# Half of the first weight quarter moved from the float32 queues to GpSimd's queue, with other warm-up matmuls

## The chip, the cores and the metric

One core of one Trainium2 chip. The metric is the device time of one execution in microseconds (us). The kernel before takes 903.51 us in the median of 3 runs (903.43 to 903.68). TensorE multiplies, VectorE (DVE), ScalarE (ACT) and GpSimd (POOL) do the rest, and SyncE (SP) issues transfers. SP and ACT have each a queue of transfers that move data as it is (q1 and q10 in the profile); GpSimd has one that can change the type on the way (q0).

## The reference: what is computed

```python
B, S, D = (16, 2048, 1024)
xw = x @ w                      # x [B, S, D], w [D, D], float32
out[:, 0, :] = xw[:, 0, :]
for t in range(1, S):
    out[:, t, :] = decay * out[:, t - 1, :] + xw[:, t, :]
```

A matrix product, and along the sequence a recurrence with one decay for each of the 1024 output columns.

## The kernel before

**Tiles.** x is cut into 64 chunks of 512 time steps (`TL`). The contraction of 1024 is cut into 8 slices (`K`), indexed k; k = 2m + e, with m = 0 to 3 and e = 0 (even) or 1 (odd). The 1024 output columns are 8 tiles n of 128; h = 0 or 1 is the half of w with n = 0 to 3 or 4 to 7. So w has four quarters (h, e), each of 512 KB in bfloat16 and 1 MB in float32; a quarter has four pieces m of 128 partitions x 512 columns.

**x.** `load` (L101) is issued on GpSimd and converts float32 to bfloat16; a chunk comes as four transfers, one for each quarter q of the partitions. `turn` (L110, DVE) transposes blocks of 32 x 32 pairs into xw; `part` (L119, ACT or DVE copy) makes xt from it. Matmuls of the first chunks read xw itself for some k (strided pairs) and xt for the others.

**w.** `load_w` (L317) brings one quarter (h, e) as four transfers, one for each 32 partitions, into a staging tile; `settle` (L324) copies one piece m into wsb, where the matmuls read it. The first quarter (0, 0) is called for at L334, on the SP and ACT queues in turn. These do not convert, so it arrives as float32, and `settle` casts it. The other three come on GpSimd's queue (`load_part`, L359) already as bfloat16.

**The order at the start** is written by hand in `agenda[-99]` (L532); each letter with its number is one entry of `deeds`:

- M0, M1: x's chunk 0 in two cuts, time blocks 0 to 9 and 10 to 15 of 16; M2, M3: chunk 1 in two halves. Four transfers each on GpSimd.
- U0, U1, U2: the quarters (0, 1), (1, 0), (1, 1) of w. Four transfers each on GpSimd.
- W or w with i: `settle` of piece i % 4 of quarter i // 4, on DVE (W) or ACT (w). 0 to 3 are the first quarter.
- K3: `spin_on(3)`, an ACT copy of one column of x's last quarter of partitions into gate (L356), and a matmul that nobody reads, behind it.
- E0 to E3: DVE transposes of the first cut, one for each m; G or F: the copies to xt on ACT or DVE. E4 and on: the following cuts.

GpSimd carries out its transfers' issues in this order, and DVE and ACT their copies in it. A GpSimd transfer takes one of eight semaphores in turn, so the ninth issue waits for the landing of the first.

**TensorE's order.** First `spin(5, seed, wide)` (L346): matmuls on zeros in float32, each two passes (10 in the profile), written to spare, which is not read. They wait for seed, whose first column ACT writes (L337) after it has loaded its table. Then the spin of K3; then step 0 (L652): for the first cut the even k = 0, 2, 4, 6 for four tiles n each (they read xw and the first quarter of w), then the odd k (xt and U0's quarter), and the same for the second cut, then chunk 1. From there on TensorE goes through steps of one tile n and two chunks each.

Of the kernel before, what the change touches and what calls it, by code (L numbers as in the profile page):

```python
# [9 lines left out]
FP32 = mybir.dt.float32  # L10
BF16 = mybir.dt.bfloat16
# [3 lines left out]
def _ap(ap_obj: bass.AP, new_ap, extra_offset=0):  # L15
    return dataclasses.replace(
        ap_obj,
        ap=[list(p) for p in new_ap],
        offset=ap_obj.offset + extra_offset,
    )  # L20
# [5 lines left out]
def kernel(  # L26
# [26 lines left out]
    nc = tc.nc  # L53
    pin = tc.keep_in_program_order
    B, S, D = x.shape
    assert w.shape == (D, D)

    NQ = 4
    P = 32
    CQ = D // NQ  # L60
    K = CQ // P
    M = K // 2
# [3 lines left out]
    R = K // 2  # L66
    CH = D // 2
    CR = CH // NQ

    const = ctx.enter_context(tc.tile_pool(name="const", bufs=1))  # L70
# [9 lines left out]
    def quad(q):  # L80
        return slice(q * P, (q + 1) * P)
# [12 lines left out]
    def ot_tile(nj):  # L94
        return ring(sb, "ot", 4, [128, nj, CR])
# [45 lines left out]
    class Tile:  # L141
# [45 lines left out]
        def copy(self):  # L187
            self.xs = sb.tile([128, 2 * TL], FP32, name=f"xs{self.lot % 3}")[:, 0:self.T]
            size = self.T // len(self.parts())
            for i, ps in enumerate(self.parts()):  # L190
                pin(nc.scalar.copy(out=self.xs[:, i * size:(i + 1) * size], in_=ps))  # L191
# [94 lines left out]
    class Outlet:  # L286
# [8 lines left out]
        def store(self, b, t0):  # L295
# [4 lines left out]
            for j in range(0, self.nj, nj):  # L300
# [8 lines left out]

    room = [ot_tile(2 * NJ).rearrange("p j c -> p (j c)") for _ in range(2)]  # L310
    size = M * CH
    stage = {(0, 0): room[0][:, 0:size],
             (0, 1): room[0][:, size:size * 3 // 2].bitcast(BF16),
             (1, 0): room[1][:, 0:size // 2].bitcast(BF16),
             (1, 1): room[1][:, size // 2:size].bitcast(BF16)}

    def load_w(queues, h, e):  # L317
        for i, q in enumerate((0, 2, 1, 3)):
            pin(queues[i % len(queues)].dma_start(  # L319
                out=stage[h, e][quad(q)].rearrange("p (m d) -> p m d", m=M),  # L320
                in_=_ap(w, [[2 * D, P], [2 * P * D, M], [1, CH]],
                        (q * CQ + e) * D + h * CH)))

    def settle(h, e, m, copy):  # L324
        src = stage[h, e][:, m * CH:(m + 1) * CH]
        pin(copy(out=wcols[:, 2 * m + e, h],  # L326
                 in_=src.rearrange("p (q r i) -> p q r i", q=NQ, r=R)))

    wide = const.tile([128, TL], FP32, name="wide")
    idle = wide[:, 0:TL // 2].bitcast(BF16)  # L330
    spare = ring(psp, "spare", 1, [128, TL])
    rows = const.tile([128, 2, P], FP32, name="rows")
    seed = const.tile([128, 128], FP32, name="seed")
    load_w((nc.sync, nc.scalar), 0, 0)  # L334
    pin(nc.vector.memset(wide, 0.0))
    pin(nc.vector.memset(seed, 0.0))
    pin(nc.scalar.copy(out=seed[:, 0:1], in_=wide[:, 0:1]))  # L337

    gate = const.tile([128, 128], BF16, name="gate")
    pin(nc.vector.memset(gate, 0.0))  # L340

    def spin(count, by, on):
        for _ in range(count):
            pin(nc.tensor.matmul(out=spare, lhsT=by, rhs=on, start=True, stop=True))  # L344

    spin(5, seed, wide)  # L346
    H = NJ // 2
    cuts = (((0, H + 2), (H + 2, NJ)), ((0, H), (H, NJ)))
    cols = const.tile([128, 2, P], FP32, name="cols")
# [7 lines left out]
        spin(1, gate, idle)  # L357

    def load_part(i):  # L359
        load_w((nc.gpsimd,), *((0, 1), (1, 0), (1, 1))[i])  # L360

    def part_one(i, copy):
        part(i // 8, copy, i % 4, i % 4 + 1, *cuts[i // 8][i // 4 % 2])
# [1 line left out]
    def settle_one(i, copy):  # L365
        settle(i // 8, i // 4 % 2, i % 4, copy)
# [119 lines left out]
    def turn_and_load(c):  # L486
# [16 lines left out]
        "w": lambda i: settle_one(i, nc.scalar.copy),  # L503
        "M": load_half,
        "U": load_part,
        "r": await_settled,
        "E": lambda i: turn(i // 8, *cuts[i // 8][i // 4 % 2], i % 4, i % 4 + 1),
# [21 lines left out]
        "L": lambda i: load(*loads.pop(0)) if loads else None,  # L529
    }  # L530
    agenda = {
        -99: "M0 U0 M1 M2 M3 U1 U2 w0 W1 w2 W3 K3 E0 E1 G0 E2 G1 E3 F2 G3 W4 w5 W6 W7 E4 E5 G4 E6 G5 E7 F6 G7 R E8 E9 G8 E10 G9 E11 F10 G11 E12 L E13 G12 L E14 G13 E15 L F14 G15 D",  # L532
        0: "",
        1: "",
        2: "",
# [220 lines left out]
```

## Time and profile before

| what | value |
|---|---|
| median of 3 runs | 903.51 us |
| the profiled execution | 903.32 us |
| its span, first to last instruction | 901.5 us |
| granted TensorE clock, mean | 0.999 |
| TensorE busy (PE) | 894.6 us, 99% |
| weight loads (PEld) | 412.8 us, 46% |
| DVE, ACT, POOL busy | 825.8, 685.7, 656.8 us |
| read from HBM, written to it | 138.42 MB, 134.22 MB |
| first spin on TensorE | 3.21 us |
| first real matmul (even k, first cut) | 10.90 us |
| first matmul of the odd k | 13.29 us |

Times inside the execution count from the start of the span. In the timeline, a line holds the start, the length, the engine, the line of the code, the operation, the tiles (out<-in) and the count of merged instructions; the brackets hold the engine's idle time before it and what ended that. PE is a matmul, PEld a weight load. In the view of the DMA queues a row holds packets, MB, and the time of the packets as a share of 16 engines' time. A queue's MB count what is written to the destination.

### The profile page before, as it was taken

Reading aid. Unit: us, or ns where it says so; the run is one execution under the profiler, and the core shown is the slowest. Engines: PE = TensorE matmul, PEld = TensorE weight load, DVE = VectorE, ACT = ScalarE, POOL = GpSimd, SP = SyncE. Lnnn points to the kernel's source line nnn. Section 1 sums busy time; section 2 is a strip of 40 time slices with the busy share of each in tenths; the row PEclk is TensorE's granted clock in tenths of the full one; section 3 lists DMA queues with packets and bytes.
Section 4 is the critical chain, followed back from the end, with each engine's and each line's share of the span. In section 5 each row is a group of like instructions: output and inputs, shape, how many; then the busy total and the mean of one; then the engine's idle time right before and its main releaser. Section 6 shows DMA issues by size and latency. Waiting matters only on the chain.

```text
span 901.5 us, 12309 instructions
## 1 busy us (share of the span) xinstructions
PE 894.6 (99%) x4211; PEld 412.8 (46%) x4211; DVE 825.8 (92%) x633; ACT 685.7 (76%) x957; POOL 656.8 (73%) x758
## 2 busy tenths in 40 slices
PE   8999999999999999999999999999999999999998
PEld 5544444444444444444444444444444444444444
DVE  4999989999999999999998999989999999999998
ACT  4888879877877877878778778777787787787743
POOL 7887778877767768677677687777777777776532
PEclk9999999999999999999999999999999999999999
DMA  9999999999999999999999999999999999999658
GB/s 189 192 211 244 244 205 215 215 230 240 248 237 264 242 254 242 256 253 246 220 245 218 228 241 211 239 223 228 236 228 223 229 235 226 230 219 219 187 135 239
DMA packets 403182, 204.77 MB, mean 227 GB/s; under 512 B 9392, under 2 KB 402096, under 8 KB 403120
## 3 DMA queue, kind: packets, MB, share of 16 engines
q0 software_dynamic: 137024, 68.70, 57.5%
q1 hardware_dynamic: 265808, 134.77, 57.1%
q8 instruction: 33, 0.54, 0.2%
q10 hardware_dynamic: 288, 0.52, 0.2%
q14 instruction: 29, 0.24, 0.1%
HBM read 138.42 MB, written 134.22 MB: 302 GB/s over the span
## 4 chain that ended last, share of the span: by engine, by line
PE 99%; ACT 0%; ACTq 0%; DVE 0%; DVEq 0%; issue 0%
PE ps L131 97%; PE spare L131 1%; PE spare L344 1%; ACT L337 0%; PE spare L412 0%; ACTq L319 0%; PE ps L412 0%; DVE h L440 0%; ACT seed L337 0%; DVEq L751 0%
## 5 line engine op out<-in xcount | busy, mean ns | idle before, releaser
L131 PE MATMUL ps<-xt,wsb 128*128 128x512 bf16 (+2 forms) x4040 | 865.9, 377 | 0.0
L131 PEld LDWEIGHTS <-wsb 128*128 128x128 bf16 x4184 | 408.3, 98 | 477.2 <-DVE wsb L326 0.3
L205 POOL TENSOR_TENSOR xs<-h,xs 128x512 f32<-128x512 f32 (+1 forms) x190 | 242.4, 1277 | 185.5 <-ACT h L171 84.4
L191 ACT COPY xs<-ps 128x1024 f32<-128x1024 f32 (+1 forms) x190 | 188.7, 994 | 153.4 <-PE ps L131 147.2
L278 DVE STREAM_TRANSPOSE ot<-so 128x1024 f32<-128x1024 f32 (+2 forms) x264 | 300.6, 1176 | 2.7 <-POOL so L266 2.0
L266 POOL TENSOR_TENSOR so<-h,xs 128x512 f32<-128x512 f32 (+1 forms) x189 | 240.6, 1274 | 38.4 <-ACT h L171 26.2
L123 ACT COPY xt<-xw 128x2048 bf16<-128x2048 bf16 (+3 forms) x136 | 242.4, 1788 | 5.8 <-DVE xw L115 5.8
L105 POOL DMA_DIRECT2D xb<-in_x_dram x264 | 173.8, 659 | 7.6 <-DMA xb<-in_x_dram 2.8
L171 ACT ACTIVATE h<-so,dec 128x512 f32<-128x512 f32 (+1 forms) x189 | 144.7, 766 | 26.6 <-DVE so L210 23.3
L115 DVE STREAM_TRANSPOSE xw<-xb 128x2048 f32<-128x2048 f32 (+3 forms) x78 | 147.2, 1899 | 6.1 <-DMA xb<-in_x_dram 6.1
L210 DVE TENSOR_TENSOR_SCAN so<-spare,keep,xs 128x512 f32<-128x512 f32 (+1 forms) x97 | 120.0, 1240 | 27.5 <-POOL xs L205 26.9
L210 DVE TENSOR_TENSOR_SCAN so<-spare,xs 128x512 f32<-128x512 f32 x93 | 113.3, 1220 | 25.9 <-POOL xs L205 22.6
L171 ACT ACTIVATE h<-ps,dec 128x512 f32<-128x512 f32 (+1 forms) x190 | 129.6, 683 | 0.0
L229 DVE TENSOR_TENSOR_SCAN so<-dec,ps 128x1024 f32<-128x1024 f32 x34 | 76.9, 2261 | 0.8 <-ACT h L171 0.6
L229 DVE TENSOR_TENSOR_SCAN so<-dec,keep,ps 128x1024 f32<-128x1024 f32 (+2 forms) x35 | 75.5, 2156 | 0.8 <-PE ps L131 0.8
L270 ACT COPY keep<-so 128x1 f32<-128x1 f32 x136 | 25.3, 188 | 9.3 <-DVE so L229 8.7
L201 ACT COPY so<-keep 128x1 f32<-128x1 f32 x97 | 18.3, 191 | 3.3 <-DVE ot L278 3.2
L199 POOL MEMSET so<- 128x1 f32 x93 | 10.6, 115 | 3.0 <-DVE ot L278 3.0
L131 PE MATMUL spare<-xt,wsb 128*128 128x512 bf16 (+3 forms) x60 | 12.6, 329 | 0.0
L131 PE MATMUL ps<-xw,wsb 128*128 128x256 bf16 (+3 forms) x72 | 12.2, 306 | 0.0
L344 PE MATMUL spare<-wide,seed 128*128 128x512 f32 x10 | 7.4, 915 | 3.2 <-ACT seed L337 3.2
L319 POOL DMA_DIRECT2D ot<-in_w_dram x12 | 6.5, 548 | 0.7 <-issue 0.3
(43 smaller groups left out, 37.6 us busy)
## 6 DMA issues: line engine op xcount, KB each, us to landing
out_dram<-ot SPq DMA_DIRECT2D x236, 512.0 KB, 8.9
xb<-in_x_dram POOLq DMA_DIRECT2D x248, 256.0 KB, 7.4
out_dram<-ot SPq DMA_DIRECT2D x56, 128.0 KB, 2.2
out_dram<-ot SPq DMA_DIRECT2D x8, 256.0 KB, 4.8
ot<-in_w_dram POOLq DMA_DIRECT2D x12, 128.0 KB, 5.8
xb<-in_x_dram POOLq DMA_DIRECT2D x8, 128.0 KB, 4.5
out_dram<-xb SPq DMA_DIRECT2D x3, 256.0 KB
xb<-in_x_dram POOLq DMA_DIRECT2D x4, 160.0 KB, 6.6
```

What stands on the lines that cost most here:

```text
L105: pin(nc.gpsimd.dma_start(out=xb_of[c][quad(q), j0:j1], in_=_ap(x, [[D, P], [P * D, j1 - j0], [1, CQ]], (b * S + t0 + j0 * P) * D + q * CQ)))
L115: pin(nc.vector.transpose(out=dst.rearrange("p (m j i) -> p j m i", m=M, i=P)[:, j0:j1, m0:m1], in_=src.rearrange("p (j m c) -> p j m c", ...
L123: pin(copy(out=xt_of[c][:, m0:m1, :, j0 * P:j1 * P], in_=src))
L131: return pin(nc.tensor.matmul(out=ps[:, t0 % ps.shape[1]:][:, 0:t1 - t0], lhsT=lhs, rhs=rhs, start=(k == 0 and t0 == start), stop=(k == K ...
L171: pin(nc.scalar.activation(out=h[:, i * size:(i + 1) * size], in_=src, func=mybir.ActivationFunctionType.Copy, scale=dec[:, self.n:self.n ...
L191: pin(nc.scalar.copy(out=self.xs[:, i * size:(i + 1) * size], in_=ps))
L205: pin(nc.gpsimd.tensor_tensor(out=odds, in0=self.g, in1=odds, op=ALU.add))
L210: pin(nc.vector.tensor_tensor_scan(out=so[:, 3:T + 2:2], data0=squares[-1][:, n:n + 1].to_broadcast([128, T // 2]), data1=self.xs[:, 1:T:2 ...
L229: return pin(nc.vector.tensor_tensor_scan(out=so[:, t + 2:t + 2 + size], data0=dec[:, n:n + 1].to_broadcast([128, size]), data1=ps, initia ...
L266: pin(nc.gpsimd.tensor_tensor(out=self.so[:, 2:T + 2:2], in0=self.h, in1=self.xs[:, 0:T:2], op=ALU.add))
L270: pin(nc.scalar.copy(out=self.keep, in_=self.so[:, self.T + 1:self.T + 2]))
L278: pin(nc.vector.transpose(out=outlet.ot[:, :, c0:c0 + P], in_=self.so[:, 2 + t0:2 + t0 + nj * P].rearrange("p (i t) -> p i t", t=P)))
```

## The change

The first quarter of w is split by pieces. Pieces m = 0 and 1 (`early = M // 2`) still come as float32 on the SP and ACT queues at the start, now four transfers of half the size. Pieces 2 and 3 come through GpSimd as bfloat16, as a new U3 of four transfers, placed in the order between M0 and U0. The staging tile keeps its place: its first half holds the float32 pieces, its second half the bfloat16 ones.

The warm-up is 4 float32 spins (8 passes) with wide[:, 0:128] as weights instead of 5 with seed, and then 2 bfloat16 spins with gate as weights. seed shrinks to one column and its memset goes; ACT's copy into it stays (no matmul reads it any more).

In the order of the start, K2 is new (a spin behind x's third quarter of partitions), w2 and W3 become W2 (DVE) and w3 (ACT) and move behind E2, and G1 moves behind E3.

```diff
+    early = M // 2
+    first_rows = room[0][:, 0:early * CH]
-    stage = {(0, 0): room[0][:, 0:size],
+    stage = {(0, 0): room[0][:, early * CH:size].bitcast(BF16),
...
-    def load_w(queues, h, e):
+    def staged(h, e, m0, m1):
+        if (h, e) == (0, 0) and m1 <= early:
+            return first_rows[:, m0 * CH:m1 * CH]
+        return stage[h, e][:, m0 * CH:m1 * CH]
+
+    def load_w(queues, h, e, m0=0, m1=M):
         for i, q in enumerate((0, 2, 1, 3)):
             pin(queues[i % len(queues)].dma_start(
-                out=stage[h, e][quad(q)].rearrange("p (m d) -> p m d", m=M),
-                in_=_ap(w, [[2 * D, P], [2 * P * D, M], [1, CH]],
-                        (q * CQ + e) * D + h * CH)))
+                out=staged(h, e, m0, m1)[quad(q)].rearrange("p (m d) -> p m d", m=m1 - m0),
+                in_=_ap(w, [[2 * D, P], [2 * P * D, m1 - m0], [1, CH]],
+                        (q * CQ + e + 2 * P * m0) * D + h * CH)))
...
-    seed = const.tile([128, 128], FP32, name="seed")
-    load_w((nc.sync, nc.scalar), 0, 0)
+    seed = const.tile([128, 1], FP32, name="seed")
+    load_w((nc.sync, nc.scalar), 0, 0, 0, early)
     pin(nc.vector.memset(wide, 0.0))
-    pin(nc.vector.memset(seed, 0.0))
-    pin(nc.scalar.copy(out=seed[:, 0:1], in_=wide[:, 0:1]))
+    pin(nc.scalar.copy(out=seed, in_=wide[:, 0:1]))
...
-    spin(5, seed, wide)
+    spin(4, wide[:, 0:128], wide)
+    spin(2, gate, idle)
...
-        load_w((nc.gpsimd,), *((0, 1), (1, 0), (1, 1))[i])
+        load_w((nc.gpsimd,), *((0, 1), (1, 0), (1, 1), (0, 0, early, M))[i])
...
-        -99: "M0 U0 M1 M2 M3 U1 U2 w0 W1 w2 W3 K3 E0 E1 G0 E2 G1 E3 F2 G3 W4 w5 W6 W7 ...
+        -99: "M0 U3 U0 M1 M2 M3 U1 U2 w0 W1 K2 K3 E0 E1 G0 E2 W2 w3 E3 G1 F2 G3 W4 w5 W6 W7 ...
```

The last two lines are cut behind W7; what follows is the same in both.

## The prediction

> **What bounds the kernel now.** I read the page first: its chain of work that ended last, and the spinning matmuls among its groups.
>
> ```profile
> PE 99%; ACT 0%; ACTq 0%; DVE 0%; DVEq 0%; issue 0%
> L344 PE MATMUL spare<-wide,seed 128*128 128x512 f32 x10 | 7.4, 915 | 3.2 <-ACT seed L337 3.2
> ```
>
> TensorE sets the end. The list of TensorE's waits from 10 to 40 us is empty, so a change near the start is worth just what it moves the start of TensorE's unbroken stretch. Next the timeline of the first 21 us.
>
> ```profile
> 1.31 2.51 POOL L105 DMA_DIRECT2D xb<-in_x_dram  x4 [0.86 <-POOLq L740]
> 3.81 2.16 POOL L319 DMA_DIRECT2D ot<-in_w_dram  x4
> 7.88 0.57 POOL L105 DMA_DIRECT2D xb<-in_x_dram  x1 [1.91 <-DMA xb<-in_x_dram]
> ...
> 10.29 0.19 ACT L356 COPY gate<-xb 32x1 bf16<-32x1 bf16 x1 [2.11 <-DMA xb<-in_x_dram]
> 10.33 1.69 DVE L115 STREAM_TRANSPOSE xw<-xb 128x320 f32<-128x320 f32 x4 [2.50 <-DMA xb<-in_x_dram]
> ...
> 10.90 0.59 PE L131 MATMUL ps<-xw,wsb 128*128 128x320 bf16 x3
> ...
> 12.94 0.70 DVE L326 COPY wsb<-ot 128x512 bf16<-128x512 bf16 x3 [0.54 <-DMA ot<-in_w_dram]
> ...
> 13.29 0.58 PE L131 MATMUL ps<-xt,wsb 128*128 128x320 bf16 x3
> ...
> 15.00 1.16 DVE L115 STREAM_TRANSPOSE xw<-xb 128x192 f32<-128x192 f32 x4 [1.36 <-DMA xb<-in_x_dram]
> ...
> 17.71 1.42 DVE L115 STREAM_TRANSPOSE xw<-xb 128x256 f32<-128x256 f32 x4 [1.24 <-DMA xb<-in_x_dram]
> ```
>
> The first column is the start; the brackets hold the idle time before it and what ended it. Two landings stand close together. x's first part is there at 10.29 and the first real matmuls, the even k, run from 10.90; sixteen of them, 0.14 us apart, last 2.24 us, to 13.14. The odd k need U0, w's second quarter, which is there at 12.94, and start at 13.29 behind one copy. So TensorE idles 0.15 us between the two: **U0's landing, not x's, is the later bound.** After it come M1 (15.00), M2 (17.71) and M3, each just in time; TensorE's first matmul on M2 starts at 18.21, some 0.03 us later than its spacing asks.
>
> Then the DMA queues, from 1.5 to 4 us, and from 5 to 6 us (packets, MB, share).
>
> ```profile
> q1 hardware_dynamic: 149, 0.28, 61.0%
> q10 hardware_dynamic: 127, 0.25, 25.4%
> ```
>
> ```profile
> q10 hardware_dynamic: 110, 0.20, 53.1%
> q0 software_dynamic: 124, 0.06, 46.4%
> q1 hardware_dynamic: 44, 0.06, 15.6%
> ```
>
> The float32 queues (q1, q10) bring w's first quarter, 1.05 MB; half of it is through at 4.0 us. GpSimd's queue q0, whose first x was issued at 1.31, moves its first packet at 5.50, when the float32 queues run out. From there on it is never empty: the releases 10.29, 12.94, 15.00, 17.71 are one stream. A DMA of it takes by these 0.66 us (128 KB written; (12.94-10.29)/4), 0.515 us (96 KB; (15.00-12.94)/4).
>
> **The change, part by part.**
>
> 1. Float32 half as long. 0.52 MB is through at 4.0 us instead of 1.05 MB at about 5.75. When does q0 start then? Between 1.31 plus its latency on quiet queues and the old 5.50. In the trace's later packets, where q0 had run dry, the first packet came 2.1 to 2.6 us behind the issue when 430 to 570 store packets (0.22 to 0.29 MB) went by, and mostly 2.8 to 4.1 us when 1,400 to 1,940 did (0.7 to 1.0 MB). The 4.19 us here, beside 1 MB, lies on that line; for 0.52 MB it gives some 2.9 us, start 4.2, and the drained queues give 4.0. I take 4.1; ends 3.4 and 5.5.
>
> The Trainium skill, "DMA: Bandwidth & Descriptors", section "Queues, rings and completion order", says that each DMA engine round-robins between the queues that have work. By that x's stream would have shared the engines as soon as its descriptors were there, so that its 5.50 would be its own latency and would stay; the packets, none of q0 before 5.50, with no share at all, neither prove nor exclude it. It is rival B.
>
> 2. x's first part takes 5.50 to 10.29, 4.8 us, and keeps it: 4.1 + 4.8 = 8.9. Ends: it moved only 0.16, 0.14 and 0.18 MB/us from 6 to 9 us against 0.19 to 0.20 later; at 0.195 throughout it saves about 0.9 us, and if the slow stretch belongs to the clock time and not to the stream's beginning it costs about 0.4 us more.
>
> 3. The added U3, four DMAs of 64 KB written, goes on the same queue ahead of U0. By the rows above cost follows bytes (0.515 against 0.66 for 96 against 128 KB, nearly in proportion), so 0.33 each, 1.32 in all: 10.2. Upper end: as much as the 96 KB ones, 2.06.
>
> 4. U0 keeps 2.65: **12.9 instead of 12.94.** Sum: 4.1 + 4.8 + 1.32 + 2.65 = 12.87. In other words the bytes ahead of U0 are the same ones; 0.52 MB of float32 at some 0.3 MB/us (1.75 us) are read instead in 1.32 us, and starting 1.4 us earlier gives back no more. Behind U0 one copy (0.29) and 13.29 becomes about 13.2. What x gains (TensorE's first real matmul at 9.5, not 10.9) turns into idle time: k=0, 2 from 9.5, k=4, 6 behind U3 and its copies (10.2 + 0.3 on DVE, + 0.62 on ACT) to about 11.8, then 1.4 us of waiting for U0.
>
> 5. The order of copies. W2 on DVE waits for U3 with E3, F2 queued behind; w3 on ACT with G1, G3 behind. From 10.2: W2 0.3, E3 0.4, F2 0.45, done at 11.4; w3 0.62, G1 and G3 0.65 each, done at 12.2. The odd k that need them start at 13.2, so this costs nothing; if U3 came later than 11.2, G3 would be what is late next. Two float32 casts fewer (0.42 DVE, 0.62 ACT near 7 us) stood in idle time.
>
> 6. GpSimd's issues. Eight may be in flight: its ninth, 7.88, started 0.3 us after x's first landing. U3 takes slots 5 to 8, so U0's four, issued from 3.81 before, wait for x's landings: about 6.5, 7.4, 8.3, 9.1. M1 then issues at 9.6 (was 7.88), M2 at 11.9 (11.16), M3 at 14.2 (13.8). Needed by the stream: U0 10.2, M1 12.9, M2 15.0, M3 17.7, so the leads are 3 us or more, against 2.1 to 2.6 of latency on quiet queues. Nothing is paid; were 3.8 us needed, M2 would be 0.8 late. U1, U2 and the later x loads catch up.
>
> 7. The spins. They start behind wide (1.40) instead of ACT's copy behind its table load (3.21). Eight float32 passes instead of ten, 0.855 us each while the clock is low:
>
> ```profile
> 8.49 0.34 PEld L344 LDWEIGHTS spare<-wide,seed 128*128 128x128 f32 x1 [0.52 <-issue]
> 9.18 0.19 PEld L344 LDWEIGHTS spare<-wide,seed 128*128 128x128 f32 x1 [0.35 <-issue]
> 9.61 0.19 PEld L344 LDWEIGHTS spare<-wide,seed 128*128 128x128 f32 x1 [0.24 <-issue]
> ```
>
> The spacing falls from 0.85 to 0.43 near 9.0, 5.8 us after the first pass. From 1.45 that is 7.25, inside 1.45 + 8 x 0.855 = 8.3. K2 and K3 add a spin each as x lands. All of this lies ahead of U0: no cost, no gain. The seed memset (0.17 DVE) is waited for by nobody else.
>
> The page's "TensorE: Matmul & The Clock Gate" of the Trainium skill, Part 1, has the clock rise after a fully busy window of about 3.4 us that runs freely, and fall after an idle one; by it the rise comes between 4.9 and 8.3 here, still within the spins, and no gap of 1.4 us lowers it. The 5.8 us measured agrees.
>
> Total: 12.94 to 12.87, some 0.1 us. The profiled execution took 903.32 (span 901.5 and 1.8 around it), the median of the runs is 903.51; I take 0.1 from the median: **903.4**. A measurement of this kernel tells about 0.2% (1.8 us) from no change.
>
> **Rivals.**
>
> A. The stream itself gets faster: x's slow stretch goes, or q0 starts at 3.4 between the float32 packets. For it: 0.14 MB/us is far below 0.195. Against it: the slowness stood also after the float32 queues were empty. U0, M1, M2 all move by 0.7 (0.9 at most, since x's own part is all that can shrink): 902.8. Chance 0.17.
>
> B. Slower: q0's start does not move. Place: first packet of q0. x lands at 10.3 as before, U3 1.32 behind it at 11.6, U0 at 14.27, and the unbroken stretch starts 1.3 late: 904.8. It decides from a start later than 4.2, 1 us for each us. For it: all 4.2 us could be GpSimd's first descriptors. Against: the growth of the latency with store packets. Chance 0.12.
>
> C. A lead of step 6 is too short: M2 0.8 late, 904.3. Chance 0.05.
>
> D. The clock falls in the idle time ahead of 13.2, or has not risen at 9.5. Then up to 5.8 us of matmuls run at half speed, 2.9 us lost: 906.4. It decides from how much idle time the gate bears; no row of before shows a fall between 9.0 and the end. Chance 0.06.
>
> **How the numbers follow.** The forecast keeps 0.60, its own range 903.0 to 903.9 (start 4.1 +- 0.4). The range takes in A and B: 902.6 to 904.8; left out are D and the outer edges. Faster by over 0.2% (under 901.7) would need U0 1.8 us earlier, which even all of A cannot give: 0.01. Slower by over 0.2% (over 905.3) is D: 0.06. Within: 0.93.
>
> **What would show it.** First packet of q0 near 4.1; ACT's K3 gate near 8.9; TensorE on ps<-xw near 9.5; DVE's wsb copy of U0 near 12.9 and ps<-xt near 13.2 with about 1.4 us of idle time before it put down to DVE's wsb. Wrong if the odd k start more than 0.5 us off 13.29, if TensorE waits later than that for M1 to M3, or if matmuls of 320 columns stand 0.28 us apart.

## The result, and the profile after

The changed kernel takes **906.27 us** in the median of 7 runs (904.98 to 907.11), against 903.43 (903.15 to 903.78) for the kernel before beside it: 2.84 us more, a ratio of 1.0030 (95% interval 1.0018 to 1.0042). The prediction, 903.4 with a range to 904.8, was wrong. The profiled execution took 907.07 with a span of 905.3, near the upper end of the runs and 3.75 more than the profiled one of before (903.32).

The page, as before: the chain of work that ended last by engine, and the group of spinning matmuls.

```profile
PE 97%; DMA 1%; POOL 1%; issue 0%; DVE 0%; DVEq 0%; POOLq 0%
...
L349 PE MATMUL spare<-wide 128*128 128x512 f32 x8 | 6.2, 944 | 1.5 <-DVE wide L341 1.5
```

DMA and POOL stand in the chain now with 1% each, where PE alone had 99%. TensorE's waits up to 30 us (line, what was waited for, total, times, longest) say what this is; the only wait of TensorE in the kernel before was that for seed.

```profile
PE ps L131 <- DVE wsb L332: 2.2, 1, 2.2
PE spare L349 <- DVE wide L341: 1.5, 1, 1.5
PE ps L131 <- DVE xw L115: 1.2, 1, 1.2
PE spare L349 <- ACT gate L362: 1.2, 2, 0.8
```

The first is the wait for U0, which was expected at 1.4 us. The third is new: TensorE runs dry a second time, for x's chunk 1 (M2). The timeline of the first 21 us has both.

```profile
1.31 2.49 POOL L105 DMA_DIRECT2D xb<-in_x_dram  x4 [0.86 <-POOLq L746]
...
3.79 2.11 POOL L326 DMA_DIRECT2D ot<-in_w_dram  x4
...
6.73 0.56 POOL L326 DMA_DIRECT2D ot<-in_w_dram  x1 [0.83 <-DMA xb<-in_x_dram]
...
9.44 0.19 ACT L362 COPY gate<-xb 32x1 bf16<-32x1 bf16 x1 [0.62 <-DMA xb<-in_x_dram]
9.49 1.30 DVE L115 STREAM_TRANSPOSE xw<-xb 128x320 f32<-128x320 f32 x3 [3.86 <-DMA xb<-in_x_dram]
9.65 0.54 POOL L326 DMA_DIRECT2D ot<-in_w_dram  x1 [0.28 <-DMA xb<-in_x_dram]
...
10.05 0.59 PE L131 MATMUL ps<-xw,wsb 128*128 128x320 bf16 x3
...
10.18 7.23 POOL L105 DMA_DIRECT2D xb<-in_x_dram  x12
...
14.29 0.70 DVE L332 COPY wsb<-ot 128x512 bf16<-128x512 bf16 x3 [2.38 <-DMA ot<-in_w_dram]
14.64 0.58 PE L131 MATMUL ps<-xt,wsb 128*128 128x320 bf16 x3 [2.16 <-DVE wsb L332]
...
16.35 1.16 DVE L115 STREAM_TRANSPOSE xw<-xb 128x192 f32<-128x192 f32 x4 [1.36 <-DMA xb<-in_x_dram]
...
20.42 1.42 DVE L115 STREAM_TRANSPOSE xw<-xb 128x256 f32<-128x256 f32 x4 [2.59 <-DMA xb<-in_x_dram]
...
20.92 0.84 PE L131 MATMUL ps<-xw,wsb 128*128 128x256 bf16 x6 [1.22 <-DVE xw L115]
```

Before, the last of these lines was

```profile
18.21 0.84 PE L131 MATMUL ps<-xw,wsb 128*128 128x256 bf16 x6
```

Read it against before in three places. The start gains 0.85: ACT's gate copy stands at 9.44 (10.29), the first real matmul at 10.05 (10.90). At U0 it has turned into a loss of 1.35: the odd k start at 14.64 (13.29). At chunk 1 the loss is 2.71: 20.92 (18.21). From there to the end of the matmuls it hardly changes (2.87). The other 0.88 of the 3.75 lies behind all work: the last store lands 2.97 us behind its issue, 2.09 before. That time is 2.1 to 3.1 in the kept traces, and 2.1 in kernels with the loss as well as without it, so it is no part of what follows. And in the left column GpSimd issues U0 from 6.73 to 9.65, where it was done with it by 6, and M1, M2 and M3 in one run of 12 from 10.18, where M1 had begun at 7.88.

The last column of this view of both kernels, two microseconds a row, is the rate of all DMA in GB/s. First before, then after:

```profile
12.00:14.00 2.00, 2.00 (x16) 1.18 (x14) 1.10 (x5) 1.48 (x3) 2.00 (x4) 1.00 1.42 192
14.00:16.00 2.00, 2.00 (x20) 1.58 (x18) 1.00 (x4) 0.59 (x2) 2.00 (x4) 1.00 1.45 193
16.00:18.00 2.00, 2.00 (x26) 2.00 (x25) 0.76 (x4) 0.75 (x2) 1.82 (x5) 1.00 1.45 193
18.00:20.00 2.00, 2.00 (x21) 1.72 (x19) 1.44 (x5) 1.66 (x3) 1.57 (x4) 1.00 1.43 196
```

```profile
12.00:14.00 2.00, 0.48 (x4) 0.10 (x1) 0.00 (x0) 0.67 (x2) 2.00 (x5) 1.00 1.08 129
14.00:16.00 2.00, 1.36 (x10) 0.99 (x11) 0.70 (x3) 0.62 (x1) 1.88 (x4) 1.00 1.30 160
16.00:18.00 2.00, 2.00 (x22) 1.76 (x20) 1.48 (x6) 1.24 (x3) 1.95 (x4) 1.00 1.24 140
18.00:20.00 2.00, 1.69 (x21) 1.55 (x19) 0.00 (x0) 0.10 (x1) 0.68 (x2) 1.00 1.19 138
```

Before, the stream runs at 0.19 to 0.20 MB/us from 12 to 20 us. After, it runs at 0.13 to 0.16.

### The profile page after: what moved, and what is told of

It is laid out like the page before. It is cut to its first block, busy times and chain, and to the rows that moved or that the text cites. A ratio compares the mean times of both kernels' runs of the same rounds, so it can differ in the third digit from the quotient of the medians.

```text
span 905.3 us, 12320 instructions
## 1 busy us (share of the span) xinstructions
PE 894.6 (99%) x4212; PEld 412.5 (46%) x4212; DVE 824.2 (91%) x632; ACT 685.1 (76%) x958; POOL 659.3 (73%) x762
## 4 chain that ended last, share of the span: by engine, by line
PE 97%; DMA 1%; POOL 1%; issue 0%; DVE 0%; DVEq 0%; POOLq 0%
PE ps L131 96%; DMA xb<-in_x_dram 1%; PE spare L131 1%; POOL xb L105 1%; POOL ot L326 0%; PE spare L418 0%; PE ps L418 0%; DVE h L446 0%; DVE xw L115 0%; DVEq L757 0%; DVEq L115 0%; POOLq L746 0%
## 5 line engine op out<-in xcount | busy, mean ns | idle before, releaser
L326 POOL DMA_DIRECT2D ot<-in_w_dram x16 | 8.7, 542 | 4.3 <-DMA xb<-in_x_dram 3.3
L349 PE MATMUL spare<-wide 128*128 128x512 f32 x8 | 6.2, 944 | 1.5 <-DVE wide L341 1.5
```

## The experiments

**Theory of the issues:** U3's four transfers take four of the eight slots and 2.1 us of issuing ahead of U0. So U0's issues wait for x's landings, those of M1 and M2 come late, and so do their landings; the bytes do not matter. **Rivals:** the bytes or the early start of q0 do it (the 16 DMA engines, by their landings, are 1.5 to 2 us apart in this execution, 0.5 before); or the warm-up and the clock do it.

### The warm-up alone

The kernel before with the spins of the change, its seed of one column and K2.

```diff
...
-    spin(5, seed, wide)
+    spin(4, wide[:, 0:128], wide)
+    spin(2, gate, idle)
...
-        -99: "M0 U0 M1 M2 M3 U1 U2 w0 W1 w2 W3 K3 E0 ...
+        -99: "M0 U0 M1 M2 M3 U1 U2 w0 W1 w2 W3 K2 K3 E0 ...
```

> The kernel before with the changed warm-up alone (4 float32 spins on wide, 2 bfloat16 spins, K2; no seed), all transfers as before. Both theories (late issues on GpSimd; DMA engines apart because x starts beside the float32 queues) put nothing on the warm-up: 903.4, first odd k at 13.3. If the warm-up itself cost something, a part of the 2.8 us appears here.

903.67 (11 runs), ratio 1.0004 (0.9996 to 1.0013). M1's first issue at 8.12, the odd k where they were (13.22). The warm-up isn't the loss. Two of the eleven runs, though, took 904.9 and 905.0; more on these below.

### The transfers alone

The changed kernel with the spins and the seed of before, without K2.

> The changed kernel with the warm-up of before (5 float32 spins with seed, no K2), the transfers and the order of copies as changed. Both theories: all of the loss is here, 906 (905 to 907), odd k near 14.5 and a second wait of TensorE of about 1.4 us ahead of chunk 1.

906.81 (5 runs), ratio 1.0039 (1.0025 to 1.0052): all of the loss. M1's first issue at 10.66, the odd k 1.39 late, chunk 1 3.12 late.

### Four slots without bytes

```diff
+    tiny = const.tile([128, 16], FP32, name="tiny")
+    def four_tiny(i):
+        for q in range(NQ):
+            pin(nc.gpsimd.dma_start(out=tiny[quad(q)], in_=_ap(w, [[D, P], [1, 16]], q * P * D)))
...
-        -99: "M0 U0 M1 M2 M3 ...
+        -99: "M0 q U0 M1 M2 M3 ...
```

Otherwise this is the kernel before, with the whole first quarter on the float32 queues; the four transfers bring 2 KB each.

> The kernel before with four transfers of 2 KB each (32 partitions x 64 bytes of w into a tile that nobody reads) on GpSimd's queue between M0 and U0: four slots and four issue times, next to no bytes, and the float32 queues and x's start as before. Theory of late issues: U0 waits for x's landings and M1 for the tiny ones, M1 is issued near 11 instead of 7.9, the stream runs dry, and the time rises to 905 to 907. Theory of engines driven apart by the early start: no early start here, 903.4 to 903.9.

906.54 (5 runs), ratio 1.0041 (1.0028 to 1.0054): the whole loss again. Its timeline:

```profile
3.80 2.03 POOL L366 DMA_DIRECT2D tiny<-in_w_dram  x4
...
7.88 0.58 POOL L319 DMA_DIRECT2D ot<-in_w_dram  x1 [2.06 <-DMA xb<-in_x_dram]
...
10.89 4.53 POOL L105 DMA_DIRECT2D xb<-in_x_dram  x8
...
14.66 0.58 PE L131 MATMUL ps<-xt,wsb 128*128 128x320 bf16 x3 [1.49 <-DVE wsb L326]
...
21.01 0.84 PE L131 MATMUL ps<-xw,wsb 128*128 128x256 bf16 x6 [0.51 <-DVE xw L115]
```

Four transfers that carry next to nothing take 2.03 us to issue (U3: 2.11), hold U0's issue until x's first part begins to land, and bring the odd k to 14.66 and chunk 1 to 21.01, as the change does. They are not quite free in the queue: they land from 10.07 to 10.73, 0.66 us in all, where U3's take 1.34. The next kernels do without any transfer. q0 starts late here (first packet at 5.14), so the early start isn't needed for the loss either.

### Nothing but late issues

```diff
+    heap = const.tile([128, TL], FP32, name="heap")
+    def pause(i):
+        for _ in range(i):
+            pin(nc.gpsimd.tensor_tensor(out=heap, in0=wide, in1=wide, op=ALU.add))
...
-        -99: "M0 U0 M1 M2 M3 ...
+        -99: "M0 U0 q3 M1 M2 M3 ...
```

The kernel before with additions on GpSimd between U0's issues and M1's: no transfer, byte or slot is added. Three, five and one of them:

> The kernel before with three additions of 128x512 on GpSimd (1.27 us each, nobody reads the result) between U0's and M1's issues: M1 is issued near 9.8 instead of 7.9, everything ahead of it untouched. Late issues: U0 on time (odd k at 13.3), then M1 to M3 late because the stream runs dry after U0, TensorE waits 1 to 1.5 us ahead of chunk 1: 904.5 to 905. Engines driven apart: 903.4 to 903.7.

> The kernel before with five additions (instead of three) on GpSimd between U0's and M1's issues: M1 is issued near 11.6. Three cost 1.3 us with M1 at 9.4. Late issues: 2.2 us later still, all of it lost as the queue is dry by then: 906.3 to 907. If the three had cost by something else than the time of M1's issue (GpSimd's additions beside the transfers), five cost 5/3 of it: 905.5.

> The kernel before with one addition on GpSimd between U0's and M1's issues: GpSimd is free again at 7.1 and M1 is issued when x's first landing lets it, at 7.9, as before. Late issues: no cost, 903.3 to 903.6. If the additions cost by themselves (three cost 1.3): 903.8.

Three: 904.67 (11 runs), ratio 1.0015 (1.0006 to 1.0024). Five: 907.25 (5 runs), 1.0045 (1.0031 to 1.0059). One: 903.50 (11 runs), 1.0000 (0.9992 to 1.0009). With one, M1 still issues at 7.65, when x's first landing frees its slot. With three:

```profile
6.07 3.35 POOL L366 TENSOR_TENSOR heap<-wide 128x512 f32<-128x512 f32 x3
...
9.36 7.21 POOL L105 DMA_DIRECT2D xb<-in_x_dram  x12
...
13.81 0.58 PE L131 MATMUL ps<-xt,wsb 128*128 128x320 bf16 x3
...
19.45 0.84 PE L131 MATMUL ps<-xw,wsb 128*128 128x256 bf16 x6 [0.58 <-DVE xw L115]
```

M1 issued 1.48 later than before puts chunk 1 1.24 later (19.45 against 18.21). Of that, 0.52 stands already at the odd k, since x itself landed 0.51 later in this execution: on its last DMA engine, 1.4 us behind the middle ones (0.3 before), which stays unexplained. With five, M1 issues at 11.65 and chunk 1 starts 3.28 late, though U0 came 0.54 early. Late issues alone are enough. (Five cost 0.25 more than the most that was expected.)

### Half the bytes in as many slots

```diff
-    early = M // 2
+    early = 3
...
-    stage = {(0, 0): room[0][:, early * CH:size].bitcast(BF16),
+    stage = {(0, 0): room[0][:, size // 2:size].bitcast(BF16),
```

One piece instead of two through U3: four transfers of 32 KB.

> The change with three pieces as float32 and one alone (m = 3) through U3, still four transfers, of 32 KB each: half of the moved bytes, all four slots and issue times. Late issues: the loss stays, 905.5 to 906.8. If the loss went with the moved bytes, it halves: 904.8.

907.01 (5 runs), ratio 1.0036 (1.0023 to 1.0048), a little over what was expected. Four of the five runs show a granted clock of 0.997 or 0.998 besides (more on this below); the one at 1.000 takes 906.26, still 2.8 us more than before. Half the bytes, all of the loss.

### As many bytes in fewer slots

The changed kernel, with the quarter halved by partitions and not by pieces: quarters q = 0 and 1 of the partitions come as float32, 2 and 3 through U3 in two transfers of 128 KB; the copies to wsb work on half the partitions each (V, v: the lower half).

```diff
-    load_w((nc.sync, nc.scalar), 0, 0, 0, early)
+    load_w((nc.sync, nc.scalar), 0, 0, (0, 1))
...
-        load_w((nc.gpsimd,), *((0, 1), (1, 0), (1, 1), (0, 0, early, M))[i])
+        load_w((nc.gpsimd,), *((0, 1), (1, 0), (1, 1), (0, 0, (2, 3)))[i])
...
-        ... K2 K3 E0 E1 G0 E2 W2 w3 E3 G1 F2 G3 W4 w5 ...
+        ... w2 W3 K2 K3 E0 E1 G0 V0 v1 E2 V2 v3 E3 G1 F2 W4 w5 G3 ...
```

> The change with its half cut by partitions: quarters 0 and 1 of the partitions of w's first quarter as float32 on SP and ACT (two transfers), quarters 2 and 3 as bfloat16 in a U3 of two transfers of 128 KB. The same bytes on the same queues at the same time, two slots and two issue times fewer on GpSimd. Late issues: U0's first two are issued at once, M1 near 8.8 instead of 10.2, so at least half of the 2.8 us comes back: 903.6 to 905. DMA engines driven apart by the early start: nothing comes back, 906 to 907.

904.07 (11 runs, 903.46 to 905.56), ratio 1.0007 (0.9998 to 1.0015). M1's first issue at 8.68; the rate stays at 186 to 203 GB/s from 8 to 22 us. Most of the loss is gone. The profiled execution, its slowest, lost time in another way:

```profile
11.50:15.00 3.50, 3.50 (x15) 1.97 (x14) 2.32 (x8) 2.35 (x4) 3.50 (x7) 0.51 1.41 192
```

The number before the last two is the granted clock: 0.51 from 11.5 to 15 us, in the midst of the even k. Of the other ten runs one more has a lower clock (905.04, at 0.998); one as long has not (905.08, at 1.000). So the next kernel is the same with the five spins and the seed of before.

> The version with U3 in two transfers, with the longer warm-up of before (5 float32 spins with seed, to about 10.4 us) instead of the changed one. The profile of that version showed TensorE's clock at half from 11.57 to 14.98, and its times went from 903.5 to 905.6. Theory: GpSimd's late issues were most of the change's loss, and what was left there is that fall of the clock in TensorE's idle time: here no fall, 903.4 to 904.0 with no execution over 904.6. If two slots still cost by themselves: 904.1 or more.

903.83 (11 runs), ratio 1.0005 (0.9996 to 1.0014).

```profile
8.42 0.57 POOL L105 DMA_DIRECT2D xb<-in_x_dram  x1 [0.40 <-DMA xb<-in_x_dram]
...
10.74 0.60 PE L131 MATMUL ps<-xw,wsb 128*128 128x320 bf16 x3 [0.33 <-DVE wsb L332]
...
13.36 0.58 PE L131 MATMUL ps<-xt,wsb 128*128 128x320 bf16 x3
```

M1 issues at 8.42 and the odd k start at 13.36, 0.07 later than before. The same half of w goes the same way as in the change, with q0's first packet at 3.86, and costs nothing that the runs can tell from none. It gains nothing either. One of its runs took 905.07 at a clock of 1.000, where none was expected over 904.6; that one is not explained. Last, with quarter 3 alone through GpSimd, in one slot:

> One quarter of the partitions alone moved to GpSimd (one transfer of 128 KB, one slot), the other three as float32, the warm-up of before. Late issues: M1 about 0.3 to 0.8 later than before, its lead still 4 us, no cost; the bytes ahead of U0 are the same, so 903.2 to 903.7, no gain over the kernel before.

903.54 (11 runs), ratio 1.0001 (0.9992 to 1.0010).

### Without U3

The changed kernel without U3: zeros stand in the place of pieces 2 and 3, so this kernel leaves out half of the first quarter's part of the product.

```diff
...
+    pin(nc.vector.memset(room[0][:, early * CH:size], 0.0))
...
-        -99: "M0 U3 U0 M1 M2 M3 ...
+        -99: "M0 U0 M1 M2 M3 ...
```

> The changed kernel without U3: pieces 2 and 3 of w's first quarter are not loaded (zeros stand in their place, so part of the product is left out); float32 half as long, x's early start, warm-up and copies as changed. Slots and issue times on GpSimd as before the change. Late issues: x at 9.4, U0 near 11.6, every later landing about 1 us earlier than before the change: 902.2 to 902.8. Engines driven apart by the early start: the landings still end 1 us behind the median engine, and the time stays at 904 or more.

902.86 (11 runs), ratio 0.9994 (0.9985 to 1.0002).

```profile
7.16 0.57 POOL L105 DMA_DIRECT2D xb<-in_x_dram  x1 [1.19 <-DMA xb<-in_x_dram]
...
17.61 0.84 PE L131 MATMUL ps<-xw,wsb 128*128 128x256 bf16 x6
```

M1 issues 0.7 earlier, chunk 1 starts 0.6 earlier, where 1 was expected. The DMA engines' landings are 1.5 to 2.0 us apart here as well up to M1, and q0 starts as early as in the change (3.40): neither makes the loss by itself. The spread does take a part of the gain: of M2's fourth transfer the middle engine is 1.09 earlier than before, the last 0.67. And all that an early start without U3's bytes is worth is 0.6 us, which the runs can't tell from none.

### TensorE left idle

```diff
     spin(4, wide[:, 0:128], wide)
-    spin(2, gate, idle)
...
-        -99: "... w2 W3 K2 K3 E0 ...
+        -99: "... w2 W3 E0 ...
```

The warm-up-alone kernel without the two bfloat16 spins, K2 and K3. Its last spin ends at 8.05, and TensorE idles until 10.88.

> The kernel before with the four float32 spins of the change alone: no bfloat16 spins, no spin behind x's landing. TensorE then does nothing from about 7.5 to 10.9 us. Theory: what is left of the spread of the change's times is a fall of TensorE's clock in such a gap, to half for some 3.4 us as in the profile of the version with two slots, worth up to 1.7 us: executions lie near 903.5 where it does not fall and near 905 where it does, and most fall here (median 904.5 to 905.2). Without that theory: 903.4 to 903.7, since all transfers are as before.

904.78 (11 runs, 903.20 to 906.07), ratio 1.0017 (1.0008 to 1.0026), with every transfer as before. TensorE's timeline and the clock (third number from the end) by stretches:

```profile
10.88 0.96 PE L131 MATMUL ps<-xw,wsb 128*128 128x320 bf16 x3 [2.82 <-DVE xw L115]
```

```profile
9.00:12.00 3.00, 1.12 (x5) 0.64 (x5) 1.69 (x5) 1.14 (x2) 2.37 (x5) 0.79 1.26 198
12.00:15.00 3.00, 3.00 (x16) 1.75 (x15) 1.32 (x6) 1.46 (x3) 3.00 (x6) 0.64 1.45 192
15.00:18.00 3.00, 3.00 (x29) 2.47 (x28) 1.72 (x7) 1.34 (x3) 2.68 (x6) 1.00 1.41 182
```

Three matmuls that took 0.59 together take 0.96 here: the clock is at half from 10.73 to 14.15, and chunk 1 starts at 19.53, 1.32 late. The single runs agree: ten of the eleven show a mean granted clock of 0.996 to 0.998 and take 904.46 to 906.07, the eleventh shows 0.999 and takes 903.20.

### The runs in one table

From the issue and landing records of the traces: when GpSimd issued M2's fourth transfer, and when the middle (mean of the eighth and ninth) and the last of the 16 DMA engines had landed it. "Late" is against before (13.11, 17.31, 17.59). The last column is the median of all runs, the others are of the one profiled execution, whose own time can lie elsewhere: 905.54 with three additions, 2.2 us more than before's, 1.0 of it behind the matmuls.

| kernel | issue late | landing late, middle engine | last engine | median time against before |
|---|---|---|---|---|
| without U3 | -0.70 | -1.09 | -0.67 | -0.59 |
| one addition | -0.24 | -0.49 | -0.25 | +0.11 |
| warm-up alone | -0.08 | -0.29 | +0.02 | +0.27 |
| one slot | +0.10 | -0.21 | +0.13 | +0.15 |
| two slots, old warm-up | +0.10 | +0.04 | +0.11 | +0.44 |
| two slots | +0.04 | +0.01 | -0.02 | +0.62 |
| TensorE left idle | -0.03 | -0.45 | -0.01 | +1.41 (clock) |
| three additions | +0.52 | +0.56 | +1.24 | +1.27 |
| **the change** | **+1.35** | **+1.48** | **+2.70** | **+2.84** |
| transfers alone | +1.67 | +2.36 | +3.12 | +3.41 |
| four of 2 KB | +1.70 | +2.53 | +2.80 | +3.14 |
| one piece | +1.80 | +2.26 | +2.70 | +3.56 |
| five additions | +2.52 | +2.64 | +3.28 | +3.80 |

Whatever makes the issue late by 0.5 or more, the time follows it, at one for one and more. The one marked loses time with its issues on time, by the clock. Two slots have their issues on time too; two of their eleven runs lose by the clock, and the +0.62 of the median is within what the runs can't tell from none (ratio 0.9998 to 1.0015).

## Why the prediction was wrong, step by step

**Step 6 failed:** "the leads are 3 us or more, against 2.1 to 2.6 of latency on quiet queues. Nothing is paid". Three things were wrong in it.

- *The yardstick.* 2.1 to 2.6 us is from an issue to its first packet on an empty queue. A transfer must have landed whole, on all 16 engines, behind others. The view of the DMA queues gives that beside each issue. Before, for those issued from 10.4 to 13.2 us, M1's last and M2's:

```profile
xb<-in_x_dram POOLq DMA_DIRECT2D x4, 128.0 KB, 4.4
xb<-in_x_dram POOLq DMA_DIRECT2D x1, 96.0 KB, 4.4
```

 4.4 us each, and with that they land just when TensorE needs them. At this rate M2's issues had no slack. (M1's had some: the two-slot kernels issue its first at 8.42 and 8.68 instead of 7.88, with M2's on time, and lose nothing that can be told. Where the queue had run dry, with five additions, M1's landed 2.8 to 3.3 us behind their issue; so 4.4 is the time in a running stream, not the least possible.)
- *The first of four instead of the last.* U0's fourth, forecast to issue at 9.1, had to land at 12.87, 3.8 us later; M2's fourth, at 11.9 + 3 x 0.57 = 13.6, had to land at 17.6, 4.0 later. Both are below 4.4. And 13.6 is just where three additions put it (13.62), with chunk 1 1.24 late, 0.7 of it without x's 0.52. The median of their runs lost 1.27. So the term that was put at nothing was worth 0.7 to 1.3 by its own issue times. Rival C, at 0.8, is this mechanism and of that size; it was given a chance of 0.05, since its 3.8 us were taken for a supposition, where the profile had 4.4.
- *The issue times themselves.* They follow x's landings, and these came later than in step 2: U0's fourth at 9.65 and not 9.1, M2's at 14.45 and not 13.6. U0's last engine then landed at 14.17 instead of 12.87: 0.55 from the later issue, 0.75 from 4.52 us of landing where 3.77 were there. In this execution those 4.52 are the last engine's alone: the middle one had U0's fourth at 12.51, as before. With the transfers alone and with four of 2 KB the middle one has it late as well (by 0.75 and 0.74), and the odd k are as late. M2's fourth took 5.84 us to land; here the stream had slowed to 0.14 MB/us, and the loss doubled.

Why the stream is slow then stays open. From 12 to 18 us six to eight transfers were issued and not landed on all engines (seven or eight before), five to seven by the middle engine (seven before), and still it ran at 0.13 to 0.16 MB/us, in the change, with three additions (141 and 137 GB/s from 14 to 18 us) and with four tiny transfers. The packets show where the time goes. Before, from 12 to 20 us, a packet of 512 bytes takes 60 ns and none over 171. In the change 46 of q0's 2317 packets take over 200 ns, up to 855, and what they take beyond the usual adds up to 15% of the 16 engines' time; it is 12 to 16% in all five other kernels with late issues, and 3% at most in those with M2's issues on time. The same long packets stand at the slow beginning of the stream before (17 over 200 ns from 6 to 9 us, up to 481), and with five additions right behind the gap in which the queue was empty. So they go with a stream that has just begun or is issued late; what makes them long is not shown. Nor is it settled why the last engine is 1.5 us behind the middle one in the profiled execution of the change (0.28 before): that is 1.22 of the 2.70 there, but only 0.3 to 0.8 more than before in the four kernels below it in the table, which lose more.

**Step 1** was too pessimistic: q0's first packet came at 3.43, the quiet end, not 4.1. The view of the DMA queues from 3 to 4 us:

```profile
q10 hardware_dynamic: 78, 0.13, 50.5%
q0 software_dynamic: 64, 0.03, 27.8%
q1 hardware_dynamic: 44, 0.06, 21.3%
```

q0 moves beside the float32 queues, each with its share. So rival B fell in its result: the start did move, by 2.1 us. In the rule behind it, that each DMA engine takes turns between the queues that have work (the Trainium skill, "DMA: Bandwidth & Descriptors", "Queues, rings and completion order"), this row agrees, as far as a sum over the engines can; what B added to it, that 5.50 was q0's own latency, was wrong. Nor does the latency follow step 1's line, by which 0.52 MB beside it gave 2.9 us: it was 2.1 here.

**Step 2:** x's first part took 5.9 us and not 4.8, landing at 9.36 and not 8.9. Of the bounds given there, the slow stretch belongs to the stream's beginning: before, it lay from 6.5 to 8.5; here from 3.5 to 6.5. What step 1 gave more than forecast (0.7) was more than lost here (1.1), and rival A with it: its early start at 3.4 came true, and x landed 0.85 earlier than before, but U0 and M2 did not follow.

**Steps 3 and 4,** the bytes. With its measured terms the sum is 3.43 + 5.93 + 1.34 + 3.47 = 14.17 for the last engine, instead of 4.1 + 4.8 + 1.32 + 2.65 = 12.87. So step 3 held: U3's landings stand 0.30 to 0.39 apart and cost 1.34. Steps 1 and 2 together are 0.46 over, and U0's own 2.65 is 0.82 over, behind its late issues; for the middle engine the sum is 12.51 (12.54 before), as forecast. That the same bytes ahead of U0 give no gain was right, and the two-slot kernel shows it: +0.44, within what can't be told from none. The sum counted what the queue carries and left out when it is told to.

**Step 5** held: W2 and w3 ran at 10.8, G3 was done by 12.7, and the odd k waited for U0 alone.

**Step 7** held in the profiled execution: the clock rose at 6.51, 5.05 us after the first spin, and the 320-column matmuls stood 0.14 apart. But the sentence on the skill, "no gap of 1.4 us lowers it", does not hold for every warm-up. The clock's changes stand on a grid of 3.41 us in each trace (e.g. up at 7.32, down at 10.73, up at 14.15), and what counted was TensorE's busy share of the whole cell, not one gap: it fell behind cells with 22%, 38% and 39% of matmul time (TensorE left idle, two slots, five additions) and stayed up behind all others of the first 17 us after the rise, of which the lowest had 49% (transfers alone) and 56%. In the two-slot kernel the gaps in that cell were 1.53, 0.53 and 1.00 us. The Trainium skill, "TensorE: Matmul & The Clock Gate", Part 1, has a free-running window of 3413 ns, which these traces agree with, and a fall after an idle window; here a window that was busy by more than a third still lowered it. **Rival D** is thus real for such a warm-up, at 1.3 us a fall (TensorE left idle) and not 2.9, but it isn't what the change lost in its profiled execution, whose cells had 62% and more. The mean granted clock of the single runs tells more, as one fall of 3.41 us to half costs it 0.002. The two longer runs of the warm-up alone have 0.998, the other nine 0.999 or 1.000, so a fall is very likely behind them. Of the seven runs of the change only the longest (907.11, at 0.997) shows one. The other six, at 0.999 or 1.000, run from 904.98 to 907.07; that spread is not the clock's, and stays open. Single runs with four of 2 KB, one piece and five additions show a fall too; their runs at 0.999 and 1.000 still take 906.16 to 907.75, so the loss there is not the clock's either.

The tests that the prediction named caught it: the odd k at 14.64 is 1.35 off 13.29, and TensorE waits 1.2 us for M2.

## What to carry to other kernels

For every transfer that is moved back in a software queue, compare the trace's own time from issue to full landing with the time left until it is needed, for the last of a group and not the first; an extra transfer costs a slot and an issue time whatever its size, so bytes are moved in few transfers (here two by partitions cost nothing that could be told, four by pieces cost 2.8 us). Moving bytes from one queue to another ahead of the same consumer gained nothing here: no version was measurably faster than the kernel before. Warm-up matmuls should leave no stretch of 3.4 us ahead of the real work in which TensorE is mostly idle (22 to 39% busy lowered the clock here, 49% did not). And one profile is one execution: the clock and the time differed from run to run of one kernel, so the median of the runs and their clocks are read beside it.

## What the runs showed of the hardware that was not expected

- A GpSimd transfer of 2 KB takes as much of GpSimd as one of 128 KB: four took 2.03 us to issue, against 2.11 for U3's four of 64 KB and 2.16 for U0's four of 128 KB before.
- In the first 20 us the 16 DMA engines finish one transfer mostly 0.5 us apart in the profiled execution of before and mostly 1.5 to 2.0 apart in that of the change; it differs from trace to trace, and in the kernel without U3 it is 1.5 to 2.0 up to M1 with no loss.
- Packets of 512 bytes, 60 ns each in a running stream, take up to 0.86 us in the change where the stream is issued late, and up to 0.48 in the first microseconds of the stream before.
- The first packet of q0 came 1.3 us behind its issue with the queue empty and no other beside it (five additions, issue 11.65, packet 12.96). At the start it came 2.1 us behind beside 0.5 MB of float32 (3.43), 2.5 and 2.6 where these came in two transfers (3.86, 3.94), 3.1 and 3.8 beside 0.8 MB (4.46 with one piece through U3, 5.12 with one slot), and 3.6 to 4.2 beside 1 MB (4.89 to 5.50).
- The clock moves on a grid of 3.41 us, and a cell with TensorE busy for 39% of it lowered it.
